# Input in four quarter pieces, norm weights loaded together, and two small products behind the first weight chunk

## The chip, the cores and the metric

The kernel runs on one core of a Trainium2 chip. The time is device time of one execution, in microseconds (us). The three runs of the kernel before took 946.36, 947.10 and 947.19 us; their median is 947.1 us. The profile is of one further execution.

The engines named here are TensorE (PE; PEld is its weight load), VectorE (DVE), ScalarE (ACT), GpSimd (POOL) and SyncE (SP). The names with a q behind them (SPq, ACTq) are the sequencers of these engines, which issue DMA transfers.

## The reference

A two-layer decoder trunk on 256 tokens of width 1024. Each layer is three residual steps, and each step begins with a root-mean-square norm:

```
def swiglu(x, w_gate, w_up, w_down):
    return (jax.nn.silu(x @ w_gate) * (x @ w_up)) @ w_down
...
    for layer in range(DEPTH):
        h = h + 0.5 * swiglu(rms_norm(h, ffn1_norm[layer]), ffn1_w_gate[layer], ffn1_w_up[layer], ffn1_w_down[layer])
        hn = rms_norm(h, mix_norm[layer])
        h = h + (ab_mixer(hn, ...) if layer % 2 == 0 else c_mixer(hn, ...))
        h = h + 0.5 * swiglu(rms_norm(h, ffn2_norm[layer]), ffn2_w_gate[layer], ffn2_w_up[layer], ffn2_w_down[layer])
    return rms_norm(h, final_norm)
```

The hidden width of the SwiGLU steps is 2816. The mixer of layer 0 is windowed attention beside a spatial gating unit, that of layer 1 is blocked attention. All numbers are float32. The change touches only the beginning of the first SwiGLU step of layer 0: the loading of x, its transposition, the norm weights, and the products with the first four weight chunks.

## The kernel before

**Weights as a stream.** All weights go through one list of chunks in the order of their use (`Stream`, L49). A chunk is 1 MB: for the gate and up matrices 8 row blocks of 128 (k = 0 to 7, the contraction over 1024) by 256 columns. Chunk 0 is the first 256 columns of the gate matrix, chunk 1 those of the up matrix, and so on in turn. A chunk is loaded into a `raw` tile through the SP queue (L72); there are three such tiles. The first chunk comes in four transfers of 256 KB (two row blocks each), the next three chunks in two transfers, all later ones in one. ACT and DVE then split it into a rounded part `whi` (L105, on ACT) and the remainder `wlo` (L106, on DVE). A product of two float32 numbers is made of three matmuls: L224 (hi by hi), L225 (hi of the weight by lo of the input) and L226 (lo of the weight by hi of the input). For one chunk that is 8 k times 2 column halves times 3 = 48 matmuls of 128 by 256.

**Heads.** For some chunks (`again`, L167; here numbers 1, 3 and 5 of the first SwiGLU step) the split lays out the first three row blocks in another order: their left halves lie behind all other blocks, their right halves in front (`reset`, L108 to L111). Such a chunk is said to have a head. Its split is made of four pieces for each engine instead of two.

**The beginning.** `begin` (L375) is written as a schedule by hand: each engine does its work in the order of the program. It issues the transfers, runs six small matmuls of zeros on PE (`heat`, L396 to L399), transposes the weights of the first norm (`turn_gains(0)`, L404, copied to `gT` on DVE at L405) and then works through chunk 0 in four parts of two row blocks. I call these parts 0 to 3. For each part the input must be transposed on PE (L423: four transposes into one PSUM bank `px[i]`), scaled with the norm weight and split into `xTh` (L259, ACT) and `xTl` (L262, DVE), and a quarter of the weights be split (L105 and L106 with 512 columns). Then 12 matmuls follow on PE: two row blocks times two column halves times three.

The x tile is loaded in two halves of 512 columns, each with one transfer per 128 tokens. The order in the SP queue is x half 0 (two transfers), weight quarters 0 and 1, x half 1 (two transfers), weight quarters 2 and 3, chunk 1, chunk 2. The transposes of half 0 (eight) stand ahead of part 0, those of half 1 (eight) ahead of part 1. Within a part, the order of the program is xTh and xTl of the first row block, then the weight split, then xTh and xTl of the second row block.

The norm weights come in three tiles `gr`, each with both layers of one kind. The first is loaded through the ACT queue (L390) ahead of everything else on ACT, the other two through the SP queue behind chunk 2 (L411). These two are transposed after chunk 2 (L505 to L507), just ahead of the matmuls of chunk 3.

**After the beginning.** The other chunks follow in the order of the stream. The tokens' norm factors are applied after the products, on the rows; they are spread over partitions by a transpose and a small matmul (`spread`, L312 and L313) after chunk 4.

## Time and profile before

| | |
|---|---|
| Median of three runs | 947.1 us (946.36 to 947.19) |
| The profiled execution, time | 947.28 us |
| Its span from the first to the last instruction | 945.6 us |
| PE busy | 935.2 us, 7,685 matmuls |
| DVE busy | 609.2 us |
| ACT busy | 502.2 us |
| First real matmul of chunk 0 starts | 7.17 us |
| First matmul of chunk 1 starts | 14.48 us |
| First matmul of chunk 4 starts | 31.67 us |

Times in the profile count from the first instruction. The profiled execution took 0.18 us more than the median, and 1.7 us of its time lie outside its span. A row of the timeline gives the start, the length, the engine, the line, the operation, the tiles, the shapes and how many instructions the row stands for; behind it in brackets stands the time that the engine was idle ahead of it, and what ended that. Matmuls overlap: a matmul of 128 by 256 is listed with 0.28 us, but the next one starts some 0.115 us after it.

### The profile page before, as it was taken

Reading aid. Unit: us, or ns where it says so; the run is one execution under the profiler, and the core shown is the slowest. Engines: PE = TensorE matmul, PEld = TensorE weight load, DVE = VectorE, ACT = ScalarE, POOL = GpSimd, SP = SyncE. Lnnn points to the kernel's source line nnn. Section 1 sums busy time; section 2 is a strip of 40 time slices with the busy share of each in tenths; the row PEclk is TensorE's granted clock in tenths of the full one; section 3 lists DMA queues with packets and bytes.
Section 4 is the critical chain, followed back from the end, with each engine's and each line's share of the span. In section 5 each row is a group of like instructions: output and inputs, shape, how many; then the busy total and the mean of one; then the engine's idle time right before and its main releaser. Section 6 shows DMA issues by size and latency. Waiting matters only on the chain.

```text
span 945.6 us, 18144 instructions
## 1 busy us (share of the span) xinstructions
PE 935.2 (99%) x7685; PEld 912.3 (96%) x7685; DVE 609.2 (64%) x879; ACT 502.2 (53%) x787; POOL 93.5 (10%) x116
## 2 busy tenths in 40 slices
PE   9999999999999999999999999999999999999997
PEld 8999999988999999999999999999999999999886
DVE  6766656677876665655765665567787865665543
ACT  7745444468676544444554544455786755544431
POOL 0000000034400000000000000004684000000000
PEclk9999999999999999999999999999999999999999
DMA  9866555665446656656756655656544476555521
GB/s 295 286 193 207 169 187 182 224 220 178 135 134 199 202 180 198 193 158 210 223 180 183 208 189 169 199 185 214 175 138 135 134 221 202 178 180 200 202 89 44
DMA packets 153537, 174.86 MB, mean 185 GB/s; under 512 B 3008, under 2 KB 142192, under 8 KB 153456
## 3 DMA queue, kind: packets, MB, share of 16 engines
q1 hardware_dynamic: 151888, 171.54, 56.7%
q10 hardware_dynamic: 1568, 2.17, 0.7%
q8 instruction: 60, 0.98, 0.4%
q14 instruction: 21, 0.17, 0.0%
HBM read 172.65 MB, written 1.05 MB: 184 GB/s over the span
## 4 chain that ended last, share of the span: by engine, by line
PE 91%; DVE 5%; ACT 2%; issue 1%; DMA 1%; POOL 0%; SPq 0%; POOLq 0%; ACTq 0%
PE bank L225 28%; PE bank L224 28%; PE bank L226 28%; DVE wlo L106 2%; PE bank L549 2%; PE bank L546 2%; PE bank L545 2%; PE bank L698 1%; DMA raw<-in_ffn_w_gate 1%; PE bank L677 0%; PE bank L676 0%; ACT whi L105 0%; DVE xTl L262 0%; PE bank L295 0%; POOL rsg L233 0%
## 5 line engine op out<-in xcount | busy, mean ns | idle before, releaser
L105 ACT ACTIVATE whi<-raw 128x1024 fp32r<-128x1024 f32 (+4 forms) x352 | 331.2, 985 | 369.8 <-issue 287.5
L106 DVE TENSOR_TENSOR wlo<-raw,whi 128x1024 fp32r<-128x1024 f32 (+4 forms) x352 | 390.7, 1142 | 132.4 <-ACT whi L105 131.3
L224 PE MATMUL bank<-xTh,whi 128*128 128x256 f32 x1632 | 453.1, 278 | 0.0
L225 PE MATMUL bank<-xTl,whi 128*128 128x256 f32 x1632 | 451.6, 277 | 0.2 <-DVE xTl L262 0.2
L226 PE MATMUL bank<-xTh,wlo 128*128 128x256 f32 x1632 | 451.3, 277 | 0.2 <-DVE wlo L106 0.2
L225 PEld LDWEIGHTS bank<-xTl,whi 128*128 128x128 f32 x1632 | 306.4, 188 | 0.9 <-DVE xTl L262 0.8
L226 PEld LDWEIGHTS bank<-xTh,wlo 128*128 128x128 f32 x1632 | 306.6, 188 | 0.6 <-DVE wlo L106 0.6
L224 PEld LDWEIGHTS bank<-xTh,whi 128*128 128x128 f32 x1632 | 306.4, 188 | 0.1
L224 PE MATMUL bank<-hTh,whi 128*128 128x256 f32 x528 | 145.7, 276 | 0.0
L225 PE MATMUL bank<-hTl,whi 128*128 128x256 f32 x528 | 145.7, 276 | 0.0
L226 PE MATMUL bank<-hTh,wlo 128*128 128x256 f32 x528 | 145.7, 276 | 0.0
L226 PEld LDWEIGHTS bank<-hTh,wlo 128*128 128x128 f32 x528 | 99.1, 188 | 0.0
L224 PEld LDWEIGHTS bank<-hTh,whi 128*128 128x128 f32 x528 | 99.1, 188 | 0.0
L225 PEld LDWEIGHTS bank<-hTl,whi 128*128 128x128 f32 x528 | 99.1, 188 | 0.0
L486 DVE TENSOR_TENSOR hm<-gs,bank 128x512 f32<-128x512 f32 x44 | 30.2, 688 | 80.0 <-PE bank L226 79.6
L483 DVE TENSOR_TENSOR gs<-bank,row 128x512 f32<-128x512 f32 x44 | 30.0, 690 | 47.7 <-PE bank L226 47.7
L224 PE MATMUL bank<-mixh,whi 128*128 128x256 f32 x128 | 35.3, 281 | 0.0
L225 PE MATMUL bank<-mixl,whi 128*128 128x256 f32 x128 | 35.1, 277 | 0.0
L226 PE MATMUL bank<-mixh,wlo 128*128 128x256 f32 x128 | 35.0, 277 | 0.0
L628 POOL MEMSET zeros<- 128x256 f32 x2 | 0.6, 312 | 341.9 <-DVE x L273 341.9
L690 POOL TENSOR_SCALAR pr<-pr,rl 128x128 f32<-128x128 f32 (+1 forms) x32 | 32.9, 1041 | 15.4 <-DVE rl L686 15.1
L233 POOL TENSOR_TENSOR rstd<-ms,half_neg 128x2 f32<-128x2 f32 x6 | 5.1, 851 | 269.3 <-DVE ms L297 252.6
(139 smaller groups left out, 908.7 us busy)
## 6 DMA issues: line engine op xcount, KB each, us to landing
raw<-in_ffn_w_gate SPq DMA_DIRECT2D x42, 1024.0 KB, 5.3
raw<-in_ffn_w_up SPq DMA_DIRECT2D x42, 1024.0 KB, 5.4
raw<-in_ffn_w_down SPq DMA_DIRECT2D x35, 1024.0 KB, 5.1
raw<-in_c_w_in SPq DMA_DIRECT2D x12, 1024.0 KB, 5.2
raw<-in_ab_w_in SPq DMA_DIRECT2D x10, 1024.0 KB, 5.2
raw<-in_ffn_w_down SPq DMA_DIRECT2D x12, 768.0 KB, 4.4
raw<-in_ab_w_out SPq DMA_DIRECT2D x4, 1024.0 KB, 5.1
raw<-in_c_w_out SPq DMA_DIRECT2D x4, 1024.0 KB, 5.0
```

What stands on the lines that cost most here:

```text
L105: nc.scalar.activation(hi, r, AF.Copy)
L106: nc.vector.tensor_sub(lo, r, hi.bitcast(F32))
L224: nc.tensor.matmul(p, sh, mh, start=start, stop=False)
L225: nc.tensor.matmul(p, sh, ml, start=False, stop=False)
L226: nc.tensor.matmul(p, sl, mh, start=False, stop=stop)
L483: nc.vector.tensor_mul(g, both(pg), twice(norm["row"]))
L486: nc.vector.tensor_mul(hm, g, both(pu))
L545: nc.tensor.matmul(banks[t, h], sh, w[0][kw][:, cs], start=k == 0, stop=False)
L546: nc.tensor.matmul(banks[t, h], sh, w[1][kw][:, cs], start=False, stop=False)
L549: nc.tensor.matmul(banks[t, h], sl, w[0][kw][:, cs], start=False, stop=k == FT - 1)
L690: engine.tensor_scalar(pr[:, cs], pr[:, cs], rl[:, b : b + 1], None, op0=ALU.mult)
L698: nc.tensor.transpose(tp[:, i * 128 : (i + 1) * 128], pr[:, i * 128 : (i + 1) * 128], ident)
```

## The change

- x is one tile of 128 by 2 by 1024. It is loaded in four transfers of 256 KB, each with 256 columns of all 256 tokens. Each transfer stands directly ahead of the weight quarter with the same row blocks.
- All three tiles of norm weights are loaded through the ACT queue at the start, and the second and third are transposed right after the first four transposes of x.
- Each part has its own four transposes (`turn_x`). Those of part i + 1 stand on PE directly ahead of the matmuls of part i.
- Within a part the order is both xTh, both xTl, then the weight split.
- The second group of small matmuls of zeros has two instead of four.
- After the last matmul of chunk 0 PE makes a transpose and a small matmul on a tile of zeros, whose result nobody reads.
- Chunk 3 has no head any more. Chunks 1 and 5 keep theirs.

```
-HEAT0, HEAT1 = 6, 4
+HEAT0, HEAT1 = 6, 2
...
-    add_ffn(a["ffn1_w_gate"][0], a["ffn1_w_up"][0], a["ffn1_w_down"][0], again=(1, 3, 5))
+    add_ffn(a["ffn1_w_gate"][0], a["ffn1_w_up"][0], a["ffn1_w_down"][0], again=(1, 5))
...
-        xr = [fp.tile([128, D], F32, name=f"xr{t}") for t in range(NT)]
+        xr = fp.tile([128, NT, D], F32, name="xr")
 
         def load_x(i):
-            if i % 2 == 0:
-                h = i // 2
-                for t in range(NT):
-                    nc.sync.dma_start(xr[t][:, h * 512 : (h + 1) * 512],
-                                      x[t * 128 : (t + 1) * 128, h * 512 : (h + 1) * 512])
+            cs = slice(i * S, (i + 1) * S)
+            nc.sync.dma_start(xr[:, :, cs], x[:, cs].rearrange("(t p) c -> p t c", p=128))
...
-        nc.scalar.dma_start(*grs[0])
+        for g in grs:
+            nc.scalar.dma_start(*g)
...
-        for g in grs[1:]:
-            nc.sync.dma_start(*g)
         heat(HEAT0)
         turn_gains(0)
...
+        def turn_x(i):
+            for k in (2 * i, 2 * i + 1):
+                for t in range(NT):
+                    c = k % 2 * S + t * 128
+                    nc.tensor.transpose(px[i][:, c : c + 128], xr[:, t, k * 128 : (k + 1) * 128], ident)
+
+        turn_x(0)
+        for i in (1, 2):
+            turn_gains(i)
+        heat(HEAT1)
         for i in range(4):
-            if i < 2:
-                for t in range(NT):
-                    for k in range(4 * i, 4 * i + 4):
-                        c = k % 2 * S + t * 128
-                        nc.tensor.transpose(px[k // 2][:, c : c + 128], xr[t][:, k * 128 : (k + 1) * 128], ident)
-                if i == 0:
-                    heat(HEAT1)
             src = both(px[i])
-            nxt.hi(2 * i, src[:, 0])
-            nxt.lo(2 * i, src[:, 0])
+            for j in range(2):
+                nxt.hi(2 * i + j, src[:, j])
+            for j in range(2):
+                nxt.lo(2 * i + j, src[:, j])
             next(parts)
-            nxt.hi(2 * i + 1, src[:, 1])
-            nxt.lo(2 * i + 1, src[:, 1])
+            if i < 3:
+                turn_x(i + 1)
             w = st.parts[0]
...
+        e = bank()
+        nc.tensor.transpose(e[:, :128], warm, ident)
+        nc.tensor.matmul(e[:, 128:S], warm, ident, start=True, stop=True)
         for _ in parts:
             pass
...
-                if phase == 0 and n == 2:
-                    turn_gains(1)
-                    turn_gains(2)
```

More of the change, by code (lines that the diff above doesn't have):

```diff
@@ L444, in begin @@
         for t in range(NT):
-            xs = [xr[t][:, h * 512 : (h + 1) * 512] for h in range(2)]
+            xs = [xr[:, t, h * 512 : (h + 1) * 512] for h in range(2)]
             nc.scalar.activation(junk[:, 0], xs[0], AF.Square, scale=1.0 / math.sqrt(D), accum_out=s[:, 0, t : t + 1])
@@ L455, in begin @@
         st.free()
-        return p, turn_gains
+        return p
     def ffn(phase):
@@ L493, in ffn @@
                     with tc.manual_schedule():
-                        p, turn_gains = begin(fp)
+                        p = begin(fp)
                 else:
```

## The prediction

> **What bounds the kernel now.** I read the page's busy shares first, then the timeline of the first 32 us engine by engine, then the windows, to see how fast PE runs where it doesn't wait.

> ```profile
> PE 935.2 (99%) x7685; PEld 912.3 (96%) x7685; DVE 609.2 (64%) x879; ACT 502.2 (53%) x787; POOL 93.5 (10%) x116
> ```

> PE is the bound, busy in 935.2 of 945.6 us. An edit gains only where PE waits, or where its matmuls come slower than they can. All edits lie ahead of chunk 4 (31.67 us), and behind it PE paces the rest, so I add up how much earlier or later chunk 4 begins. PE's rows at the start:

> ```profile
> 1.10 2.93 PE L399 MATMUL bank<-warm 128*128 128x128 f32 x12 [1.10 <-DVE warm L392]
> 4.18 1.11 PE L423 MATMUL bank<-ident,xr 128*128 128x128 f32 x4
> 7.17 0.39 PE L224 MATMUL bank<-xTh,whi 128*128 128x256 f32 x1
> 7.90 0.39 PE L226 MATMUL bank<-xTh,wlo 128*128 128x256 f32 x1 [0.23 <-DVE wlo L106]
> 9.18 1.04 PE L423 MATMUL bank<-ident,xr 128*128 128x128 f32 x8
> 9.97 0.37 PE L224 MATMUL bank<-xTh,whi 128*128 128x256 f32 x1
> 11.43 0.28 PE L224 MATMUL bank<-xTh,whi 128*128 128x256 f32 x1
> 11.81 0.39 PE L226 MATMUL bank<-xTh,wlo 128*128 128x256 f32 x1
> 14.48 0.28 PE L224 MATMUL bank<-xTh,whi 128*128 128x256 f32 x1
> 31.67 0.28 PE L224 MATMUL bank<-xTh,whi 128*128 128x256 f32 x1
> ```

> Part 0 starts at 7.17 and its third matmul, the first to use wlo, waits until 7.90. From there to the part's end (9.18, the next transposes) are 1.28 us. Part 1 runs from 9.97 to 11.43, 1.46 us without a wait. Part 2 again waits for its wlo, until 11.81. Chunk 1 begins at 14.48. So it is the chain from x over ACT and DVE to wlo that paces parts 0 and 2:

> ```profile
> 5.92 0.47 ACT L259 ACTIVATE xTh<-bank,gT 128x256 fp32r<-128x256 f32 x1 [3.19 <-PE bank L423]
> 7.02 0.82 ACT L259 ACTIVATE xTh<-bank,gT 128x256 fp32r<-128x256 f32 x2
> 8.66 0.47 ACT L259 ACTIVATE xTh<-bank,gT 128x256 fp32r<-128x256 f32 x1 [0.30 <-DVE xTl L262]
> 10.04 0.48 ACT L259 ACTIVATE xTh<-bank,gT 128x256 fp32r<-128x256 f32 x1 [0.90 <-PE bank L423]
> 10.41 0.62 ACT L105 ACTIVATE whi<-raw 128x512 fp32r<-128x512 f32 x1
> 7.76 0.87 DVE L262 SCALAR_TENSOR_TENSOR xTl<-bank,gT,xTh 128x256 fp32r<-128x256 f32 x2
> 8.55 0.68 DVE L106 TENSOR_TENSOR wlo<-raw,whi 128x512 fp32r<-128x512 f32 x1
> 13.50 2.71 DVE L106 TENSOR_TENSOR wlo<-raw,whi 128x384 fp32r<-128x384 f32 x4
> ```

> In part 2 the chain took 1.77 us from the start of the first xTh (10.04) to the matmul with wlo (11.81). The row at 8.66 matters for the new order: the second xTh of a part stood idle until xTl of the first was done. They share no data, only the PSUM bank they read. Two readers of one bank from two engines go one after the other.

> The windows show PE at two paces:

> ```profile
> 15.60:25.60 10.00, 10.00 (x87) 10.00 (x86) 8.21 (x15) 9.12 (x18) 1.58 (x1) 1.00 1.01 315
> 27.30:36.90 9.60, 9.60 (x87) 9.60 (x87) 7.00 (x10) 5.18 (x6) 0.00 (x0) 1.00 1.05 341
> 38.70:194.70 156.00, 156.00 (x1379) 156.00 (x1379) 99.81 (x114) 75.96 (x97) 2.60 (x5) 1.00 0.61 196
> ```

> The columns are the window, its length, busy time and count of PE, PEld, DVE, ACT and POOL, the granted clock, DMA share and GB/s. Two matmuls of each count were already running at the window's start. In chunks 1 and 2 they follow each other every 10.00/85 = 0.118 us, from chunk 3 on every 156/1377 = 0.113 us, at the same clock and with PE never idle. The quick pace begins where small products broke the stream ahead of a chunk with a head:

> ```profile
> 25.66 0.28 PE L226 MATMUL bank<-xTh,wlo 128*128 128x256 f32 x1
> 25.87 0.29 PE L404 MATMUL bank<-ident,gr 16*128 16x16 f32 x2
> 26.31 0.28 PE L225 MATMUL bank<-xTl,whi 128*128 128x256 f32 x1
> 27.14 0.28 PE L226 MATMUL bank<-xTh,wlo 128*128 128x256 f32 x1
> 300.61 0.28 PE L226 MATMUL bank<-xTh,wlo 128*128 128x256 f32 x1
> 300.73 0.27 PE L312 MATMUL bank<-ident,wide 128*128 128x128 f32 x1
> 301.19 0.28 PE L225 MATMUL bank<-xTl,whi 128*128 128x256 f32 x1
> ```

> The first nine matmuls behind the break, those of the head's three row blocks, still come slowly (26.31 to 27.14 is 0.119 each). The spread ahead of chunk 5, which has a head too, begins the 38.70 window's quick stretch. Chunk 1 has a head but no break, and stays slow.

> **The change, part by part.** (1) *Transfers.* Each row below is one transfer; the last number is the time from issue to landing.

> ```profile
> 0.79 0.86 SPq L384 DMA_DIRECT2D xr<-in_x  x2
> 1.70 0.94 SPq L72 DMA_DIRECT2D raw<-in_ffn_w_gate  x2
> xr<-in_x SPq DMA_DIRECT2D x1, 256.0 KB, 2.5
> xr<-in_x SPq DMA_DIRECT2D x1, 256.0 KB, 3.9
> raw<-in_ffn_w_gate SPq DMA_DIRECT2D x1, 256.0 KB, 4.8
> gr<-in_ffn_norm ACTq DMA_DIRECT2D x1, 8.0 KB, 2.2
> 9.32 1.30 SPq L411 DMA_DIRECT2D gr<-in_mix_norm  x1
> ```

> The first three slots landed at 0.79 + 2.5 = 3.3, about 1.2 + 3.9 = 5.1 and 1.70 + 4.8 = 6.5. Sizes and count stay, so I give the new pieces these times: x0 3.3, weights 0 5.1, x1 6.5. Half-length rows could shift each by some tenths either way, which the slack below covers. The two norm tiles leave SP (1.30 us of issue for the first alone); the next issue there waits for a raw tile anyway, so nothing is gained. On ACT they add two issues (estimate 0.4 us each, from half of 0.86) ahead of its first work. With 2.2 us to land they are there by 4.5, before PE asks at 5.1. If they took 5 us, PE would stand until 6.6, which still costs little, since part 0 waits for wlo until 7.7.

> (2) *The chain in the new order.* The first four transposes stay at 4.18 to 5.29, being behind the heat and the first norm weights, not behind x. xTh can begin at 5.33 instead of 5.92, as no second set of transposes lies between. Then: second xTh 0.35 later (0.82 - 0.47), done at 0.82; whi from 0.72 to 1.35, covered; first xTl only at 0.85, because of the bank; second at 1.24 (0.39 apart by 0.87 - 0.48); wlo from 1.63 to 2.32; the matmul at 2.37. That is 0.60 more than 1.77. Part 0: 5.33 + 2.37 = 7.70, end 8.98 (9.18 before). The transposes of x1 at 6.5 and the first two matmuls fit ahead of it.

> (3) *Transposes between the parts.* Four cost 4 x 0.11 = 0.44 us on PE ((1.04 - 0.27)/7 each); the bank is read 0.64 us after their start, and matmuls can follow after 0.36. Before, the x of parts 2 and 3 was transposed early; now x2 waits behind part 0 and x3 behind part 1. Part 1: start 8.98 + 0.36 = 9.34, its wlo ready at about 9.4, end 9.34 + 1.46 = 10.80. Part 2: xTh at 8.98 + 0.64 = 9.62, wlo matmul 11.99, end 13.27. Part 3: xTh at 10.80 + 0.64 = 11.44, wlo matmul 13.81, end 15.09. Chunk 1 would thus begin 15.09 - 14.48 = **0.61 us later**. If the bank didn't hold the first xTl back, wlo would come 0.24 sooner per part (it would then wait for whi at 1.39), and two such steps in a row leave about +0.1; with the old 1.77 the result is -0.56, worked out below. I take +0.61, since the wait at 8.66 was seen.

> (4) *The two small products* have the form of the spread: 301.19 - 300.61 = 0.58, less two normal steps of 0.113, is **+0.35 us**. With wlo pieces for chunk 1 done about 0.3 later than before (from 13.50 on, 2.71 long), so by 16.5, and chunk 1 starting at 15.4, no piece is late.

> (5) *The norm transposes ahead of chunk 3 go*: 26.31 - 25.66 = 0.65, less two steps of 0.118, **-0.42 us**. At their new place they run while PE waits for x1. So do the two heats; the two dropped cost and gain nothing there.

> (6) *Pace.* If break and head work as at 26 and 37 us, 39 matmuls of chunk 1 and 48 of chunk 2 come every 0.113 instead of 0.118: 87 x 0.0043 = **-0.37 us**. The nine slow ones move from chunk 3 to chunk 1. Chunk 3 without a head keeps the pace, as chunks 6 and on do in the 38.70 window. Its split in fewer pieces is off PE's path. If the pace doesn't turn, this term is +0.42 instead (below).

> Sum: 0.61 + 0.35 - 0.42 - 0.37 = +0.17, so 947.28 + 0.17 = 947.45 for an execution like the profiled one. That one stood 0.18 above the median, so I say **947.3 us**: no change. For this kernel 0.2%, 1.9 us, is about what a measurement can tell from none.

> **Rivals.** *A, the front gains.* If the chain keeps its 1.77 us, part 0's wlo matmul comes at 7.13 (now held by x1's transposes), part 0 ends at 8.41, part 2's is at 8.41 + 0.64 + 1.77 = 10.82, part 1 ends at 8.41 + 0.36 + 1.46 = 10.23, part 3's is at 12.64, and chunk 1 begins at 13.92: -0.56 in place of +0.61, in all -1.0, 946.1. For it speaks that x0 and its weights come sooner; against it the new order of xTl.

> *B, the pace doesn't turn until the spread ahead of chunk 5.* Then 39 + 3 x 48 = 183 matmuls cost 0.0043 more each: +0.79, 948.1. For it speaks chunk 1 today; against it, today it has no break.

> *C, the clock comes late.* The first heats lie (2.93 - 0.42)/11 = 0.23 us apart and the first transposes last 0.42; at 9.18 a transpose lasts 0.27. PE is slow until somewhere between. If half the heat doesn't bring the full clock before part 0, ten matmuls at 0.23 instead of 0.118 make part 0 end 1.1 us later, and all behind it: 948.4. Against it speaks that PE has work nearly throughout from 1.1 to 6.4 in both. [...]

> *D, slower than the bound.* The slow pace outlasts the head of chunk 5 too. It decides if the first 60 matmuls behind the spread don't come down to 0.113. Then another 1377 to 195 us cost 0.0043 each, 5.9: 954.0. Against it: in today's trace that break and head turned it.

> **How the numbers follow.** My forecast 0.53, A 0.20, B 0.12, C 0.06, D 0.04, anything else 0.05. The range 946.1 to 948.5 reaches from A over B to C. Only D and mixtures of B and C with a late transfer pass +1.9 us, which I give 0.10 with part of the unnamed; for faster by that much no term has room, which leaves a surprise (0.04). Within 0.2%: 0.86.

> **What would show it.** Part 0's wlo matmul near 7.7, those of parts 2 and 3 near 12.0 and 13.8, each behind DVE wlo; first xTl of a part behind the second xTh; chunk 1 some 0.6 + 0.35 later; windows of chunks 1 and 2 at 0.113; no break at chunk 3; chunk 4 near 31.8. The forecast is wrong if part 3's wlo comes before 13 (A), if chunks 2 to 4 stay at 0.118 (B), if matmuls of part 0 are 0.2 apart (C), or if anything behind chunk 5 changes pace.

## The result and the profile after

The changed kernel takes 948.3 us (median of 20 runs, 947.16 to 950.30) beside 946.5 us for the kernel before on the same chip (20 runs, 946.02 to 947.54). The ratio is 1.0019, with a 95% interval of 1.0013 to 1.0026: slower, by a little less than the 0.2% that I had called the bound. The forecast was 947.3. What strikes first is the spread, 3.1 us against 1.5.

The profiled execution took 948.32 us, with a span of 946.6. PE does as much work as before. From the page:

```profile
PE 935.3 (99%) x7684; PEld 912.6 (96%) x7684; DVE 608.8 (64%) x877; ACT 501.8 (53%) x785; POOL 93.7 (10%) x116
```

PE's timeline at the start of the changed kernel (L402 is the transpose of norm weights, L397 the heat, L419 the transposes of x, L441 and L442 the two small products):

```profile
6.05 0.26 PE L402 MATMUL bank<-ident,gr 16*128 16x16 f32 x1 [0.54 <-DMA gr<-in_ffn_norm]
7.25 1.06 PE L419 MATMUL bank<-ident,xr 128*128 128x128 f32 x4
8.53 0.41 PE L226 MATMUL bank<-xTh,wlo 128*128 128x256 f32 x1
9.17 0.41 PE L226 MATMUL bank<-xTh,wlo 128*128 128x256 f32 x1
9.57 0.28 PE L225 MATMUL bank<-xTl,whi 128*128 128x256 f32 x1
10.17 0.60 PE L419 MATMUL bank<-ident,xr 128*128 128x128 f32 x4
13.20 0.39 PE L226 MATMUL bank<-xTh,wlo 128*128 128x256 f32 x1 [0.34 <-DVE wlo L106]
15.07 0.39 PE L226 MATMUL bank<-xTh,wlo 128*128 128x256 f32 x1 [0.23 <-DVE wlo L106]
16.36 0.27 PE L441 MATMUL bank<-ident,warm 128*128 128x128 f32 x1
16.81 0.28 PE L225 MATMUL bank<-xTl,whi 128*128 128x256 f32 x1
33.05 0.28 PE L224 MATMUL bank<-xTh,whi 128*128 128x256 f32 x1
```

Two things were not in the sum. PE stood 0.54 us for the third norm tile. And the matmuls of part 0 up to 9.17 last 0.41 us, those from 9.57 on 0.28: the full clock came at about 9.5 us, when it had come at about 6.3 in the profile before (9.52 and 6.27 in the clock record of the traces). Chunk 4 begins at 33.05, 1.38 later than before (31.67).

DVE in the same stretch:

```profile
6.34 0.17 DVE L403 COPY gT<-bank 128x16 f32<-128x16 f32 x1 [0.62 <-PE bank L402]
6.43 0.88 DVE L262 SCALAR_TENSOR_TENSOR xTl<-bank,gT,xTh 128x256 fp32r<-128x256 f32 x2
7.23 0.68 DVE L106 TENSOR_TENSOR wlo<-raw,whi 128x512 fp32r<-128x512 f32 x1
11.68 0.87 DVE L262 SCALAR_TENSOR_TENSOR xTl<-bank,gT,xTh 128x256 fp32r<-128x256 f32 x2 [0.99 <-ACT xTh L259]
12.47 0.68 DVE L106 TENSOR_TENSOR wlo<-raw,whi 128x512 fp32r<-128x512 f32 x1
```

The two xTl of a part start together behind both xTh, and wlo behind them, as forecast. The first xTl, however, also stands behind the copy of the third norm tile's transpose (6.34). The behaviour of the stream behind the break is read from the windows:

```profile
17.90:38.30 20.40, 20.40 (x183) 20.40 (x182) 14.86 (x19) 14.11 (x20) 1.58 (x1) 1.00 0.99 316
40.00:196.00 156.00, 156.00 (x1379) 156.00 (x1378) 99.86 (x114) 76.11 (x97) 2.60 (x5) 1.00 0.62 198
```

Less the two already running, that is 20.40/181 = 0.113 us a matmul from chunk 1 to the spread, where chunks 1 and 2 had 0.118 before. Behind the spread it is 156/1377 = 0.113, as before. So in this execution the quick pace began behind the two small products, as they were meant to make it.

### The profile page after: what moved, and what is told of

It reads as the page before. It is cut to its first block, busy times and chain, and to the rows that moved or that the text cites. A ratio compares the mean times of both kernels' runs of the same rounds, so it can differ in the third digit from the quotient of the medians.

```text
span 946.6 us, 18144 instructions
## 1 busy us (share of the span) xinstructions
PE 935.3 (99%) x7684; PEld 912.6 (96%) x7684; DVE 608.8 (64%) x877; ACT 501.8 (53%) x785; POOL 93.7 (10%) x116
## 3 DMA queue, kind: packets, MB, share of 16 engines
HBM read 172.65 MB, written 1.05 MB: 183 GB/s over the span
## 4 chain that ended last, share of the span: by engine, by line
PE 91%; DVE 5%; ACT 2%; issue 1%; DMA 0%; POOL 0%; ACTq 0%; POOLq 0%
PE bank L224 28%; PE bank L225 28%; PE bank L226 28%; DVE wlo L106 2%; PE bank L548 2%; PE bank L551 2%; PE bank L547 2%; PE bank L700 1%; PE bank L679 0%; PE bank L678 0%; DVE xTl L262 0%; DMA gr<-in_ffn_norm 0%; ACT whi L105 0%; PE bank L295 0%; POOL rsg L233 0%
## 5 line engine op out<-in xcount | busy, mean ns | idle before, releaser
L105 ACT ACTIVATE whi<-raw 128x1024 fp32r<-128x1024 f32 (+4 forms) x350 | 330.9, 990 | 370.1 <-issue 287.6
L106 DVE TENSOR_TENSOR wlo<-raw,whi 128x1024 fp32r<-128x1024 f32 (+4 forms) x350 | 390.1, 1147 | 133.3 <-ACT whi L105 132.3
L224 PE MATMUL bank<-xTh,whi 128*128 128x256 f32 x1632 | 453.3, 278 | 0.0
L225 PE MATMUL bank<-xTl,whi 128*128 128x256 f32 x1632 | 451.7, 277 | 0.2 <-DVE xTl L262 0.2
L226 PE MATMUL bank<-xTh,wlo 128*128 128x256 f32 x1632 | 451.3, 277 | 0.6 <-DVE wlo L106 0.6
L225 PEld LDWEIGHTS bank<-xTl,whi 128*128 128x128 f32 x1632 | 306.8, 188 | 0.9 <-DVE xTl L262 0.7
L226 PEld LDWEIGHTS bank<-xTh,wlo 128*128 128x128 f32 x1632 | 306.6, 188 | 1.0 <-DVE wlo L106 1.0
L224 PEld LDWEIGHTS bank<-xTh,whi 128*128 128x128 f32 x1632 | 306.9, 188 | 0.0
L224 PE MATMUL bank<-hTh,whi 128*128 128x256 f32 x528 | 145.7, 276 | 0.0
L225 PE MATMUL bank<-hTl,whi 128*128 128x256 f32 x528 | 145.7, 276 | 0.0
L226 PE MATMUL bank<-hTh,wlo 128*128 128x256 f32 x528 | 145.7, 276 | 0.0
L226 PEld LDWEIGHTS bank<-hTh,wlo 128*128 128x128 f32 x528 | 99.1, 188 | 0.0
L225 PEld LDWEIGHTS bank<-hTl,whi 128*128 128x128 f32 x528 | 99.1, 188 | 0.0
L224 PEld LDWEIGHTS bank<-hTh,whi 128*128 128x128 f32 x528 | 99.1, 188 | 0.0
L224 PE MATMUL bank<-mixh,whi 128*128 128x256 f32 x128 | 35.2, 280 | 0.0
L225 PE MATMUL bank<-mixl,whi 128*128 128x256 f32 x128 | 35.1, 277 | 0.0
L226 PE MATMUL bank<-mixh,wlo 128*128 128x256 f32 x128 | 35.0, 277 | 0.0
L692 POOL TENSOR_SCALAR pr<-pr,rl 128x128 f32<-128x128 f32 (+1 forms) x32 | 32.9, 1042 | 15.4 <-DVE rl L688 15.1
```

The source lines that it names most:

```text
L105: nc.scalar.activation(hi, r, AF.Copy)
L106: nc.vector.tensor_sub(lo, r, hi.bitcast(F32))
L224: nc.tensor.matmul(p, sh, mh, start=start, stop=False)
L225: nc.tensor.matmul(p, sh, ml, start=False, stop=False)
L226: nc.tensor.matmul(p, sl, mh, start=False, stop=stop)
L692: engine.tensor_scalar(pr[:, cs], pr[:, cs], rl[:, b : b + 1], None, op0=ALU.mult)
```

## The experiments

All ratios are to the kernel before, run on the same chip. Two questions were to be answered: how much the new order within a part costs (steps 2 and 3), and what makes the clock come late (rival C), the pause for the norm tile or chance.

**Feeding PE in the pause.**

```
         turn_x(0)
+        heat(4)
         for i in (1, 2):
             turn_gains(i)
```

> The changed kernel with four more small matmuls of zeros on PE between the first transposes of x and the second and third norm transposes, so that PE has work while the third norm tile is on its way. Theory 1 (the clock comes late because PE stood from 5.3 to 6.05 us for that tile): the quick matmuls begin near 6.3 instead of 9.5, part 0 ends near 9.1 instead of 10.17, chunk 1 starts about 1.0 us sooner, the time falls from 0.19% above the kernel before to 0.05 to 0.1% above it, and the runs lie closer together. Theory 2 (the clock comes when its window happens to end, whatever PE does in that pause): as the changed kernel, quick matmuls at 9.5 in the profile or scattered over the runs, 0.19% above. Theory 3 (the order within a part is the whole loss): no difference to the changed kernel either, with the quick clock early or late.

Ratio 1.0012 (1.0003 to 1.0022), 10 runs from 946.92 to 948.37. The profile's full clock came at 5.9, but part 0's wlo matmul was no sooner, 8.53 again. The heats pushed the norm transposes back, and the copies of these stand ahead of xTl in DVE's queue:

```profile
6.57 0.29 PE L402 MATMUL bank<-ident,gr 16*128 16x16 f32 x2
6.84 0.26 DVE L403 COPY gT<-bank 128x16 f32<-128x16 f32 x2 [2.37 <-PE bank L402]
7.01 0.87 DVE L262 SCALAR_TENSOR_TENSOR xTl<-bank,gT,xTh 128x256 fp32r<-128x256 f32 x2
8.53 0.38 PE L226 MATMUL bank<-xTh,wlo 128*128 128x256 f32 x1 [0.35 <-DVE wlo L106]
```

So the early norm transposes cost through DVE as well as through PE. The gain of 1 us that theory 1 named didn't come, though the clock did: chunk 1 began at 16.22, 0.4 sooner than in the changed kernel (16.61). The runs did draw together, to 1.5 us.

**The norm transposes as the break.**

```
-HEAT0, HEAT1 = 6, 2
+HEAT0, HEAT1 = 6, 4
...
         turn_x(0)
-        for i in (1, 2):
-            turn_gains(i)
...
-        e = bank()
-        nc.tensor.transpose(e[:, :128], warm, ident)
-        nc.tensor.matmul(e[:, 128:S], warm, ident, start=True, stop=True)
+        for i in (1, 2):
+            turn_gains(i)
```

> The changed kernel with the second and third norm transposes moved from the front to the place of the two small products behind chunk 0 (which go), and four heats as before. Theory 1: no wait for the third norm tile, PE busy with heats until x1 lands at 6.6, quick matmuls from about 6.3, part 0 ends near 9.1; the break costs 0.42 instead of 0.35 us, the pace of chunks 1 to 3 is 0.113; 0.05 to 0.1% above the kernel before. Theory 2: as the changed kernel, 0.19% above.

Ratio 1.0022 (1.0013 to 1.0031); a miss. The clock was early (4.8) and part 0's wlo matmul came at 7.56, but the time was lost again behind the break:

```profile
15.29 0.25 DVE L403 COPY gT<-bank 128x16 f32<-128x16 f32 x2 [1.67 <-PE bank L402]
16.07 0.39 PE L226 MATMUL bank<-xTh,wlo 128*128 128x256 f32 x1 [0.32 <-DVE wlo L106]
```

The copies of the norm transposes stood 1.67 us for PE, with the split of chunk 1 behind them in DVE's queue. From chunk 1 (15.25) to chunk 4 (32.94) it took 17.69 us; in the changed kernel it was 33.05 - 16.61 = 16.44. The same idea on the kernel before:

```
-        nc.scalar.dma_start(*grs[0])
+        for g in grs:
+            nc.scalar.dma_start(*g)
...
-        for g in grs[1:]:
-            nc.sync.dma_start(*g)
...
+        for i in (1, 2):
+            turn_gains(i)
         for _ in parts:
             pass
...
-                if phase == 0 and n == 2:
-                    turn_gains(1)
-                    turn_gains(2)
```

Chunk 3 has no head here either.

> The kernel before with one part of the change alone: all norm tiles through the ACT queue, and the second and third norm transposes moved from ahead of chunk 3 to ahead of chunk 1, where they are the break; chunk 3 without a head. Front as before. Forecast's step 6: chunks 1 to 4 at 0.113 us a matmul, 87 x 0.0043 = 0.37 us less, the break's cost unchanged at 0.42: 0.04% below the kernel before, chunk 4 at 31.3 instead of 31.67. If the pace doesn't turn at chunk 1, 0.04 to 0.09% above.

Ratio 1.0023 (1.0013 to 1.0034); also a miss, for the same reason. Its timeline around the break, and the window behind it:

```profile
14.84 0.29 PE L405 MATMUL bank<-ident,gr 16*128 16x16 f32 x2
15.11 0.26 DVE L406 COPY gT<-bank 128x16 f32<-128x16 f32 x2 [1.30 <-PE bank L405]
15.28 2.49 DVE L106 TENSOR_TENSOR wlo<-raw,whi 128x384 fp32r<-128x384 f32 x4
15.89 0.39 PE L226 MATMUL bank<-xTh,wlo 128*128 128x256 f32 x1 [0.32 <-DVE wlo L106]
17.22 0.38 PE L226 MATMUL bank<-xTh,wlo 128*128 128x256 f32 x1
```

```profile
17.60:37.00 19.40, 19.40 (x168) 19.40 (x167) 15.70 (x20) 13.68 (x20) 1.58 (x1) 1.00 0.96 300
```

On DVE the copy of the norm transposes stood 1.30 us for PE, and the split of chunk 1, next in its queue, began behind it, at 15.28. PE then waited at 15.89 and once more near 17.2, and the matmuls went on at 19.40/166 = 0.117 us until the spread. The pace had turned in the changed kernel's window, behind a break whose result nobody reads. In the kernel before it turned ahead of chunk 3 (0.118 to 0.113) behind a break with a reader, so the reader alone doesn't decide it.

**The two small products alone**, put into the kernel before behind chunk 0:

```
+        e = bank()
+        nc.tensor.transpose(e[:, :128], warm, ident)
+        nc.tensor.matmul(e[:, 128:S], warm, ident, start=True, stop=True)
```

> The kernel before with one part of the change alone: the two small products of zeros between chunks 0 and 1. Forecast's steps 4 and 6: chunk 1's first matmuls 0.35 us later, 87 matmuls of chunks 1 and 2 at 0.113 instead of 0.118 (-0.37): chunk 4 at 31.6 to 31.7 as before, time within 0.03%. If the break doesn't turn the pace, +0.35 us, 0.04%.

Ratio 1.0000 (0.9991 to 1.0009). Its timeline and its window:

```profile
14.14 0.27 PE L439 MATMUL bank<-ident,warm 128*128 128x128 f32 x1
31.28 0.28 PE L224 MATMUL bank<-xTh,whi 128*128 128x256 f32 x1
```

```profile
15.60:25.00 9.40, 9.40 (x85) 9.40 (x85) 7.24 (x13) 8.18 (x14) 1.58 (x1) 1.00 1.05 327
```

The pace is 9.40/83 = 0.113 us in chunks 1 and 2. From where chunk 1 would have begun (14.14) to chunk 4 are 17.14 us; before, they were 31.67 - 14.48 = 17.19. Here the break cost what the pace gave back, as steps 4 and 6 had it.

**The old order within a part**, with the rest of the change:

```
-            for j in range(2):
-                nxt.hi(2 * i + j, src[:, j])
-            for j in range(2):
-                nxt.lo(2 * i + j, src[:, j])
+            nxt.hi(2 * i, src[:, 0])
+            nxt.lo(2 * i, src[:, 0])
             next(parts)
+            nxt.hi(2 * i + 1, src[:, 1])
+            nxt.lo(2 * i + 1, src[:, 1])
```

> The changed kernel with the order within a part of the kernel before: xTh and xTl of the first row block, weight split, xTh and xTl of the second. Forecast's step 2: from the first xTh to the matmul with wlo 1.77 instead of 2.37 us; over parts 1 and 3 or 0 and 2 two such steps follow on each other, so chunk 1 starts 0.6 to 1.2 us sooner than in the changed kernel if the clock comes at the same time, and the time is 0.07 to 0.13% above the kernel before. If the order counts for nothing (parts bound by PE or by the transfers), 0.19% above as the changed kernel.

Median 946.45 us, ratio 1.0005 (0.9995 to 1.0014), in two groups: six runs from 945.81 to 946.56, four from 948.00 to 948.47. The median lies below the kernel before's (946.67); the upper four pull the ratio above 1. The profile is of the lower group, with the full clock at 4.9:

```profile
10.89 0.47 ACT L259 ACTIVATE xTh<-bank,gT 128x256 fp32r<-128x256 f32 x1 [0.32 <-PE bank L419]
11.92 0.69 DVE L106 TENSOR_TENSOR wlo<-raw,whi 128x512 fp32r<-128x512 f32 x1
12.66 0.39 PE L226 MATMUL bank<-xTh,wlo 128*128 128x256 f32 x1 [0.19 <-DVE wlo L106]
13.93 0.27 PE L441 MATMUL bank<-ident,warm 128*128 128x128 f32 x1
30.63 0.28 PE L224 MATMUL bank<-xTh,whi 128*128 128x256 f32 x1
```

In part 3 xTh to the wlo matmul took 12.66 - 10.89 = 1.77 us. In the changed kernel it was 2.40 (below). A second profile of the same kernel:

> The changed kernel with the old order within a part, for a second profile: either the quick group (clock before 7 us throughout, chunk 1 near 14.2, about 945.9) or the slow group, 2 us longer; in the slow group theory 1 expects the clock to be off for one window of 3.4 us (on near 4 and off near 7.5, or not on before 9).

948.62 us, near the upper group. The full clock came at 9.2, and the window from 17 to 37 shows the slow pace on top of it (20.00/170 = 0.118 us):

```profile
17.00:37.00 20.00, 20.00 (x172) 20.00 (x171) 15.91 (x20) 14.94 (x22) 1.57 (x1) 1.00 1.02 327
```

So in this profile the clock was not on before 9 us, theory 1's second alternative. The pace cost another 0.80 us up to chunk 5: 38.70 - 15.76 = 22.94 us here, 36.32 - 14.18 = 22.14 in the first profile. That is the price that rival B had (0.79). Why the same kernel ran at two paces is open. Chunk 1's split on DVE lay the same way to chunk 1's first matmul, in the first profile and in the second:

```profile
12.92 2.62 DVE L106 TENSOR_TENSOR wlo<-raw,whi 128x384 fp32r<-128x384 f32 x4
14.18 0.37 PE L224 MATMUL bank<-xTh,whi 128*128 128x256 f32 x1
14.48 2.62 DVE L106 TENSOR_TENSOR wlo<-raw,whi 128x384 fp32r<-128x384 f32 x4
15.76 0.36 PE L224 MATMUL bank<-xTh,whi 128*128 128x256 f32 x1
```

It ended 1.36 and 1.34 us behind that matmul, and PE waited for it in neither.

**Taking the clock's pause away**, from the kernel before: `HEAT1` from 4 to 0.

> The kernel before without its second group of four heats, so that PE stands from about 6.1 to 7.2 us ahead of part 0; nothing else is changed. Theory 1: a part of the runs (those whose clock window ends within or shortly behind that pause) get the clock one window later and take 1 to 2 us more, while the others stay at the time of the kernel before: runs spread over 2 us, median 0 to 0.15% above. Theory 2: no change, runs within 1 us as before.

Ratio 1.0010 (1.0001 to 1.0019), 10 runs from 946.23 to 949.38, where the kernel before ran from 946.44 to 947.70. That is the wider spread of theory 1. The windows of its profile show the clock directly (the third column from the end):

```profile
4.20:7.50 3.30, 1.93 (x12) 1.25 (x12) 1.53 (x4) 1.87 (x5) 0.00 (x0) 1.00 0.81 270
7.60:10.90 3.30, 3.30 (x17) 3.30 (x17) 1.53 (x4) 0.86 (x2) 0.00 (x0) 0.50 1.06 365
11.00:14.00 3.00, 3.00 (x27) 2.84 (x25) 2.40 (x5) 2.75 (x7) 0.00 (x0) 1.00 1.09 349
```

The full clock was there early (from 4.1 on), PE was busy for 1.93 of 3.30 us, and the clock fell to half for the next 3.4 us although PE never stopped in them. The steps of the clock lie at 4.14, 7.55 and 10.96, 3.41 us apart; that the clock goes by windows, as the theories have it, was my assumption until this run. So in this profile the pause of PE was followed by one such stretch at half clock. That is not always so: in two profiles below, PE stood 1.06 and 0.57 us in the stretch behind the grant, and the clock stayed.

How often it happens can be read from the mean granted clock of each run. It is 0.996 in this profile, with one stretch lost; otherwise it is 0.998 or 0.999. Among the kernels in which PE stands ahead of part 0, 0.996 was recorded in 3 of the 10 runs here, in 3 of the 20 of the changed kernel (949.15 to 949.76 us) and in 2 of the 10 with the old order (948.00 and 948.47). It was recorded in none of the 42 runs of the four kernels in which that pause was filled or moved (the fed pause, the norm transposes as the break, and the next two), and in none of the 33 of the kernel before. A first grant that comes late doesn't lower this mean (0.999 in the profile of record).

**Late norm transposes without a reader in front**, in both orders:

```
-HEAT0, HEAT1 = 6, 2
+HEAT0, HEAT1 = 6, 3
...
         turn_x(0)
-        for i in (1, 2):
-            turn_gains(i)
...
         e = bank()
-        nc.tensor.transpose(e[:, :128], warm, ident)
-        nc.tensor.matmul(e[:, 128:S], warm, ident, start=True, stop=True)
+        for i in (1, 2):
+            nc.tensor.transpose(e[:, i * 128 : i * 128 + 2 * KD], grs[i][0], ident[: 2 * KD, : 2 * KD])
...
         st.split_one()
+        for i in (1, 2):
+            c = i * 2 * KD
+            nc.vector.tensor_copy(gT[:, c : c + 2 * KD], e[:, i * 128 : i * 128 + 2 * KD])
```

With the old order:

> The changed kernel with the order within a part of the kernel before, three heats, and the second and third norm transposes as the break ahead of chunk 1, with their copies on DVE only behind the split of chunk 1 (no small products of zeros). PE has work from 1.1 us to the first part but for some tenths. Theory 1 (the slow group of runs of the run with the old order, 2 us longer, is those in which the clock's window held the pause for the third norm tile): no slow group, all runs within 0.6 us of each other, 0.05 to 0.1% below the kernel before. Theory 2 (the clock comes late by chance, whatever PE does): a slow group again in some 4 of 10 runs.

Median 946.56, ratio 0.9996 (0.9987 to 1.0004), 11 runs from 945.66 to 948.20, eight of them below 946.9. The group at 948 has shrunk to one run, but the runs don't lie within 0.6 us of each other, as theory 1 had it. With the changed kernel's order:

> The same with the changed kernel's order (both xTh, both xTl, then the weight split). Between this and the run with the old order lies the order alone: forecast's steps 2 and 3 give two chains of 0.60 each, 1.2 us or 0.13%. Between this and the changed kernel lie the wait for the third norm tile and the clock: theory 1 says the runs draw together (within 0.6 us) and lie 0.05 to 0.1% above the kernel before; theory 2 that they stay spread over 3 us.

Median 947.89, ratio 1.0009 (1.0000 to 1.0018), 947.00 to 948.89. The order alone is thus 947.89 - 946.56 = 1.3 us in these medians, 1.2 by the forecast. The runs lie within 1.9 us, not 0.6. The profile (948.89, the slowest) holds another wait, for x1, though its clock was early (6.5):

```profile
7.63 0.63 PE L419 MATMUL bank<-ident,xr 128*128 128x128 f32 x4 [1.06 <-DMA xr<-in_x]
```

> The changed order with late norm transposes, for a second profile. If the x1 transfer that landed at 7.6 us in its first profile was an outlier: x1 at 6.0 to 6.7, part 0's wlo matmul near 7.7 to 7.9, chunk 1 near 15.4 (forecast 15.09 + 0.42), time near 947.2. If that transfer lands late in most executions, wlo matmul again behind 8.2.

947.65 us; x1 landed at 5.8, part 0's wlo matmul came at 7.74, chunk 1 began at 15.49. So x1 was late in one of two profiles of this kernel (7.5 in the other). The new place of x1's transposes ahead of part 0 exposes such a delay.

**The changed kernel again**, twice, for the same question of clock and pause:

> The changed kernel unchanged, for a second profile. If the time is lost where the first profile lost it: third norm tile landing at 5.4 to 6.0 us and DVE's first xTl behind the copy of its transpose (theory: in every execution), quick clock either before 7 us (then chunk 1 starts near 15.4 to 15.9 and the time is 947.2 to 947.8) or near 9 to 10 us (chunk 1 at 16.6, 948.3 and more).

> The changed kernel unchanged, for a third profile, with the same two cases: quick clock before 7 us and 947.2 to 947.8, or near 9 to 10 us and 948.3 or more.

947.26 and 947.21 us. In both the full clock was there from 4.1 to 4.3 on. The first of them:

```profile
5.56 0.20 PE L402 MATMUL bank<-ident,gr 16*128 16x16 f32 x1 [0.57 <-DMA gr<-in_ffn_norm]
7.42 0.39 PE L226 MATMUL bank<-xTh,wlo 128*128 128x256 f32 x1 [0.34 <-DVE wlo L106]
9.33 0.84 ACT L259 ACTIVATE xTh<-bank,gT 128x256 fp32r<-128x256 f32 x2 [1.09 <-PE bank L419]
11.73 0.38 PE L226 MATMUL bank<-xTh,wlo 128*128 128x256 f32 x1 [0.32 <-DVE wlo L106]
13.61 0.39 PE L226 MATMUL bank<-xTh,wlo 128*128 128x256 f32 x1 [0.23 <-DVE wlo L106]
14.90 0.27 PE L441 MATMUL bank<-ident,warm 128*128 128x128 f32 x1
31.59 0.28 PE L224 MATMUL bank<-xTh,whi 128*128 128x256 f32 x1
```

The pause for the third norm tile is there again (0.57), so the late tile is no chance of the profile of record. The clock is what differs: its stretch ended at 4.1 here, ahead of the pause, and at 6.1 (9.52 - 3.41), just behind the pause, in the profile of record. The same kernel gets either, so chance decides as well as the pause.

## Why the prediction was right or wrong

The time lies in the range, and no change beyond 0.2% was the forecast. But the likeliest case was 947.3, and the median is 1.0 above it. Step by step, with the two profiles of the changed kernel that differ most in the clock:

| | forecast | full clock at 9.5 | full clock at 4.1 |
|---|---|---|---|
| part 0, wlo matmul | 7.70 | 8.53 | 7.42 |
| part 2, wlo matmul | 11.99 | 13.20 | 11.73 |
| part 3, wlo matmul | 13.81 | 15.07 | 13.61 |
| chunk 1 would begin | 15.09 | 16.36 | 14.90 |
| chunk 4 begins | 31.84 | 33.05 | 31.59 |
| time of the execution | 947.45 | 948.32 | 947.26 |

**Transfers (1): one was mis-sized, as was its price.** x1 landed at 5.5 to 6.6 in the three profiles of the changed kernel (forecast 6.5), x0 at 3.7 to 3.9 (forecast 3.3), ahead of PE's first use at 4.2. The third norm tile was put at "by 4.5"; it landed at 5.9 (issued at 1.77, 4.1 us to land) and at 5.3 and 5.4 in the other two. The row I took, 2.2 us, was that of the one small transfer that was issued first of all. I had said that a late tile "still costs little", since part 0 waits for wlo until 7.7. I missed two things. The copy of the transpose stands on DVE ahead of xTl, which the run with more heats shows at its worst. And the clock came late behind PE's pause: in the profile of record wlo was done at 7.23 + 0.68 = 7.91, and PE, at its slow clock, reached the matmul at 8.53 without a wait.

**The chain and the transposes between parts (2, 3): right.** xTh to the wlo matmul is 11.73 - 9.33 = 2.40 us where 2.37 was forecast, and 1.77 in the old order. Part 3 was forecast at 13.81 and came at 13.61 with an early clock. The pair of kernels that differ in the order differ by 1.3 us.

**Break, pace and the norm transposes ahead of chunk 3 (4, 5, 6): right.** From where chunk 1 would begin to chunk 4 the change takes 33.05 - 16.36 = 16.69 us, before 17.19: -0.50, forecast 0.35 - 0.42 - 0.37 = -0.44.

**The rivals.** A fell: the order held the chain back. Its 946.1 is where the lower group of the run with the old order lies (945.8 to 946.6), but partly by luck: A meant 1.0 us below the kernel before, and that group's median, 946.1, is 0.6 below it (946.67 on that chip). B and D fell for the profiles of the change, but B's slow pace appeared in the second profile with the old order (0.118) and in the kernel before with the norm transposes ahead of chunk 1 (0.117). C, to which I gave 0.06, is what the profile of record shows: forecast 948.4, measured 948.32, with the clock about one 3.4 us stretch late. Of the 20 runs, four lie at or below 947.5, near the two executions with an early clock (947.2 and 947.3); the median lies above. Three of the five runs above 949 lost a stretch of the clock (0.996). That the other runs at 948 and more owe it to the clock is not shown: two profiles speak for it (this one and the second one with the old order), one against (x1 late).

What step failed is thus the weighing of C. I wrote that PE "has work nearly throughout from 1.1 to 6.4 in both"; in the changed kernel it stood from 5.5 to 6.05. The clock's steps in the run without heat lie 3.41 us apart, so I take the last 3.41 us before each event. The kernel before, granted at 6.27; the changed kernel, not granted at 6.10 (3.41 ahead of its grant):

```profile
2.86:6.27 3.41, 3.41 (x16) 2.85 (x16) 0.17 (x1) 0.35 (x1) 0.00 (x0) 1.00 0.87 272
```

```profile
2.69:6.10 3.41, 2.87 (x14) 2.20 (x12) 0.35 (x2) 1.85 (x5) 0.00 (x0) 1.00 0.89 286
```

The clock column says 1.00 in both rows because it counts only what the trace records as throttled, and the two records begin with the first grant (6.27 and 9.52). PE was busy for all of the first stretch and for 2.87 us of the second. In the second profile with the old order it was 3.17 of 3.41 and no grant either. But an execution of the changed kernel was granted the clock after a stretch with 2.99 us, all of it heats but for a first transpose, so PE's busy time doesn't order these stretches. The busy time of the weight loads (PEld, the number behind PE's) does, in the profiles that follow. Ahead of a grant it was 2.85 us in the kernel before, 3.38 in the changed kernel (6.10 to 9.52), 2.77 in its second profile and 2.93 with the fed pause. Where no grant came it was 2.20 in the changed kernel (2.69 to 6.10) and 2.47 in the second profile with the old order. Later, it was 1.25 of 3.30 us ahead of the fall in the run without heat, and 1.92 of 3.30 in the second profile of the changed kernel, where the clock stayed. The number of matmuls begun in a stretch orders the first six too (13 to 15 ahead of a grant, 12 where none came), so which of the two counts is open.

Of the 3.41 us in the kernel before, 2.09 were transposes of x, which leaves 1.32, and the clock was granted at their end. In the changed kernel 1.11 were transposes, which leaves 1.76, more than before, and it was not granted. So in these two profiles the transposes counted: the rest of PE's work alone would put the two the other way round.

**The base was off, and that flattered the forecast.** It was made against a median of three runs, 947.1. In 20 runs the median of the kernel before is 946.5. The change was forecast at +0.2 us and measured at +1.8, so it was missed by 1.6 us; the base, 0.6 too high, hid part of that in the time.

The run with the two products alone gives a better base, since those cost nothing and its clock came at 4.2: chunk 4 at 31.28, time 946.65. Against it, the two executions of the changed kernel with an early clock begin chunk 4 at 31.59 and 31.40, 0.31 and 0.12 us later, where 0.17 was forecast. Their times are 0.6 longer. The rest lies behind chunk 4, where these kernels don't differ: from there to the end of the span it took 913.65, 913.96 and 914.09 us. Over all 14 profiles that stretch took 913.5 to 914.1, whatever the edit (913.5 in the profile of record); why it varies is open.

## What to carry to other kernels

Look at what a new step adds to the queue of each engine, not only to the one it runs on: a tiny copy on DVE that waited for late norm transposes (2.37 us idle with the fed pause, 1.67 and 1.30 at the breaks) held back xTl or the split behind it, while a break on PE that nobody reads cost no more than the pace gave back in the run with the two products (17.14 us to chunk 4 beside 17.19). Two engines that read one PSUM bank went one after the other, in the order of the program (in the changed kernel the first xTl on DVE began at 11.68, when ACT's second xTh had ended at 11.64), so put other work between the readers: the chain took 1.77 us that way and 2.40 without. In the first 10 us keep PE fed without a gap (with 1.93 of 3.30 us busy, one profile had half the clock for the next 3.4), and judge a change there by the spread of many runs as well as by one profile.
